# A WKV recurrence's state kept plain, with its two heads' products as two 64-row tiles

## The chip, the cores and the metric

The kernel runs on one core of a Trainium2 chip. The metric is the device time of one execution in microseconds, the median of several runs. The engines are TensorE (PE in the profile, its weight loads PEld), VectorE (DVE), ScalarE (ACT), GpSimd (POOL) and SyncE (SP, whose queue issues the DMAs). TensorE multiplies a stationary operand, loaded beforehand, with a moving one, into PSUM, which has eight banks. Its array of 128 rows by 128 columns can be divided into tiles of fewer rows (the contracted dimension, on the partitions) or columns; the profile writes the division as rows*columns.

## What is computed

A trunk of two layers on two sequences of 512 tokens with 1024 channels, in float32. Layer 0 is RWKV-7 time mixing with 16 heads of 64 channels, run forward and backward; layer 1 is a neighbourhood attention. The change concerns layer 0:

```python
def step(s, inp):                 # S is (batch, head, value, key)
    r_t, w_t, k_t, v_t, a_t, b_t = inp
    sa = jnp.einsum('bhvk,bhk->bhv', s, a_t)
    s = s * w_t[:, :, None, :] + sa[..., None] * b_t[:, :, None, :] + v_t[..., None] * k_t[:, :, None, :]
    return s, jnp.einsum('bhvk,bhk->bhv', s, r_t)
...
for d in range(2):
    xw = lerp(3 + d)
    xa = lerp(5 + d)
    w_log = -jax.nn.softplus(-(w0[d] + jnp.tanh(xw @ w1[d]) @ w2[d]).astype(f32)) - 0.5
    decay = heads(jnp.exp(-jnp.exp(w_log)))
    a = heads(jax.nn.sigmoid((a0[d] + (xa @ a1[d]) @ a2[d]).astype(f32)))
    k_d = k * (1.0 + (a - 1.0) * k_a_h)
    ys.append(_wkv7_scan(r, decay, k_d, v, -kk, kk * a, reverse=(d == 1)))
```

## The kernel before

The large products (`gemm`, L208 to L210) split each float32 operand into a high and a low part and add three products of 128x128 by 512 columns each. ACT and DVE or POOL make the parts (`halves`, L163 and L164).

The scan runs over eight blocks of four heads (two sequences, four blocks each), one after the other. A block is a chain of eight steps; a step is a chunk of 64 tokens of the forward direction and one of the backward direction (index `d`), for two pairs of heads (`g`) of two heads each (`h`). The two heads of a pair lie on partitions 0 to 63 and 64 to 127. In `scan_phase` the chain of one block runs beside the inverse of the next (`inverse`), the factors of the one after (`prep`), the end of the one before (`finish`) and the stream of large products (`stream`), in fixed shares of units. The order on each engine is then set by the framework's scheduler, and each engine works in that order.

What the change touches:

- `prep`, L475 and L476: the second, low-rank factor of decay and learning rate. `h` has the high parts of the hidden values on partitions 0 to 63 and the low parts on 64 to 127, `w2h` and `w2l` have the weights' high and low parts twice, one copy above the other. L475 multiplies 128 rows, L476 the upper 64 alone.
- `intra`, L619 to L671: what a step needs beside the state. It loads `ab` (tile `cab`: the factors a, b, k, r of four heads and both directions) and the values into `X`. ACT copies r into `Rb`, a tile of block-diagonal squares with zeros elsewhere (L637). POOL forms `bk` (L639). Then, for each direction and pair, TensorE multiplies in the whole array by `Rb` (L651), transposes `bk` (L654), and multiplies in quarters of the array for `AK` (L660, `TILES` gives the order of the quarters). DVE masks the results (L662, L665), ACT evacuates the transposes as `Tm` (L669). The PSUM tile `pf` is two banks; products with `Rb` lie in the first, transposes in the second, `AK`'s two heads in one each.
- `chain`, L673 to L756: the chain itself. The state of a pair is a block-diagonal square of 128 x 128 (`Sb`, two buffers, whose zeros are set once in `scan_phase`). A step multiplies it in the whole array (L697), adds the product of `AK` and the values (L702, half columns and half rows), copies the sums `Z` out of PSUM on ACT for direction 0 (L707) and on DVE for direction 1 (L708), multiplies by the inverse (L714), copies `X` (L716 on ACT, L717 on DVE), forms the state's increment (L722), adds it to the decayed state `WS` (DVE, L727, once for each head, and copies at L729 and L731 in the first step), forms the next `WS` (POOL, L736, once for each head), and adds the product of `R` and `X` to the outputs (L743), which ACT or DVE takes into `y` (L751, L753). The PSUM pool `zy` has two tiles of one bank, one for each direction; before the scan the large products use these banks.

Of the kernel before, what the change touches and what calls it, by code (L numbers as in the profile page):

```python
# [23 lines left out]
L = 64  # L24
# [24 lines left out]
class Trunk:  # L49
# [13 lines left out]
    NBK, NRB, NRR, NTM = 1, 2, 4, 4  # L63
# [103 lines left out]
    def sums(self, out, sel, x):  # L167
        """out = sel^T x, with sel of numbers that f32r has."""
# [12 lines left out]
    def operands(self, source):  # L181
        """The parts of KT tiles."""
# [7 lines left out]
    def weight(self, src):  # L190
        """The parts of KT blocks of P columns."""
# [10 lines left out]
    def gemm(self, w, x, tag):  # L202
        """Yields after every KT-th part; the value is the PSUM tile."""
# [11 lines left out]
    def sumsq(self, acc, x, k, eng=None):  # L215
        """Adds the squares of tile k."""
# [8 lines left out]
    def rstd(self, acc):  # L225
        """1 / sqrt(mean over the channels + eps) from the sums acc, on every partition; a PSUM tile."""
# [40 lines left out]
    def prelude(self, s):  # L267
# [5 lines left out]
        for k in range(KT):  # L273
# [5 lines left out]
            if s == 0:  # L279
                # without 1 / rms, which the products get  # L280
# [32 lines left out]
        # x w and x (mu w)  # L313
# [50 lines left out]
    def hidden(self, q, u):  # L364
        """High parts on partitions ..63, low parts on the others."""
# [17 lines left out]
    # ---------------------------------------------------------------- layer 0: r, k, v, z  # L383
    def columns(self, s, kind, x, ps=range(NP)):
        nc, sp = self.nc, self.sp
        vt, act = nc.vector, nc.scalar
        for p in ps:
# [3 lines left out]
            if kind == "z":  # L391
                # 2 silu(z)
# [21 lines left out]
            if kind == "v":  # L414
                # by token, forward and with the time reversed
# [24 lines left out]
    # ---------------------------------------------------------------- layer 0: factors of the chunks  # L440
    def prep(self, s, p):
        """Of two heads: k, a, b, r with the decays; A B^T of every chunk."""
# [26 lines left out]
        for d in range(2):  # L469
            ths = []  # L470
            for q, bias in ((d, 8 * d + p), (2 + d, 16 + 8 * d + p)):
# [4 lines left out]
                nc.tensor.matmul(ps, w2l[0:64, ws], h[0:64], start=False, stop=True)  # L476
# [20 lines left out]
            # by step of the chain, with the time reversed in the backward direction (r by token all the same);  # L497
            # of a step with e = 0: b, k, a, r, with e = 1: r, a, k, b
# [22 lines left out]
            # rows: e, half of the chunk, token; columns: the tokens of that half, then those of the other  # L521
# [68 lines left out]
        # on the first half of the tokens the inverse itself, on the second the product  # L590
# [28 lines left out]
    def intra(self, s, pb, i, wc):  # L619
        """Loads of a step, and what it needs of one chunk alone."""  # L620
# [9 lines left out]
        rb = self.Rb[self.nR % len(self.Rb)]  # L630
        self.nR += 1
        bk = None if last else t("bk", (P, 2, 2, 2, L), self.NBK)
        for d in range(2):
            self.load(ab[:, d].rearrange("p g a t -> p g (a t)"), sp["ab", s, pb][i][:, d])
            self.load(X[half(1 - e[d]), d].rearrange("p g h v -> p (g h v)"), sp["vt", s][i, pb, d].rearrange("t g c -> t (g c)"))
            for h in range(2):
                act.copy(rb[half(h), d, :, h], ab[half(h), d, :, 3 - 3 * e[d]])  # L637
# [5 lines left out]
        # R B^T and R K^T (R), B and K by token with the decay of the chunk (Tm), A K^T (AK)  # L643
        R, Tm = [], []
        AK = t("AK", (P, 2, 2, L), self.NAK)
        for d in range(2):
            fm = self.p("pf", (P, 2, T))
            f = fm[:, :, 0:256].rearrange("p x (g c) -> p x g c", g=2)
            for g in range(2):
                lhs = ab[:, d, g, 2 * e[d]:2 * e[d] + 2].rearrange("p a t -> p (a t)")  # L650
                nc.tensor.matmul(f[:, 0, g], lhs, rb[:, d, g].rearrange("p h t -> p (h t)"), start=True, stop=True)  # L651
            if not last:
                for g in range(2):
                    nc.tensor.transpose(f[:, 1, g], bk[:, d, g].rearrange("p a t -> p (a t)"), self.ident)  # L654
# [8 lines left out]
            h4 = lambda x: f[:, x].rearrange("p g (h t) -> p (g h) t", h=2)  # L663
            Rd = t("R", (P, 4, L), self.NRR)
            vt.tensor_tensor(Rd, h4(0), self.mr[d].unsqueeze(1).broadcast_to([P, 4, L]), op=ALU.mult)  # L665
            R.append(Rd.rearrange("p (g h) t -> p h g t", h=2))
            if not last:
                Td = t("Tm", (P, 4, L), self.NTM)
                act.copy(Td, h4(1))  # L669
                Tm.append(Td.rearrange("p (g h) t -> p h g t", h=2))  # L670
        return ab, X, R, Tm, AK  # L671

    def chain(self, s, pb, y):  # L673
        """The chain over the chunks, both directions at once.

        e = (step + direction) % 2 is the half of the partitions that has A S, Z and U of a direction; the other half has
        its V and outputs."""
# [9 lines left out]
        for i in range(NCH):  # L687
# [622 lines left out]
```

## Time and profile before

| | |
|---|---|
| median of 3 runs | 1995.89 us (1985.74 to 1996.47) |
| span of the profiled execution | 1996.9 us |
| mean granted clock of TensorE | 0.940 |
| packets of DMA, bytes | 219240, 333.88 MB |
| HBM read and written | 166 GB/s over the span |

The profile is of one execution. A row of a group gives the line in the kernel, the engine, the operation, the tiles (out<-in), the shapes, the number of instructions, busy time and mean duration of one, and the idle time of the engine just before them with what ended most of it. A float32 product with float32 operands stands as two instructions, a float32r product and a transpose as one. The end of a matmul is modelled and matmuls overlap, so the distance of starts tells more than a duration. A line of waits names the engine that waited and, behind the arrow, the instruction that ended the wait.

### The profile page before, as it was taken

The numbers are of one execution on the slowest core, as the hardware profiler recorded it, in microseconds if no ns is written. First come the engines' busy times: TensorE is split into PE (matmuls) and PEld (weight loads), VectorE is DVE, ScalarE is ACT, GpSimd is POOL, SyncE is SP. The second block draws the span as 40 slices with busy tenths as digits, with TensorE's granted clock in tenths as the row PEclk, the third lists the DMA queues.
The fourth block names the chain that finished last, engine by engine and source line by source line (L and its number), as shares of the span: only waits on it lengthen the run. The fifth ranks groups of instructions, "written<-read, shape, count | busy, mean of one in ns | idle before, by whom it ended". The sixth has DMA issues, their size and how long they took to land.

```text
span 1996.9 us, 41739 instructions
## 1 busy us (share of the span) xinstructions
PE 1834.5 (92%) x15968; PEld 1390.7 (70%) x15968; DVE 1330.7 (67%) x2513; ACT 1012.7 (51%) x2198; POOL 874.4 (44%) x996
## 2 busy tenths in 40 slices
PE   7899977899889899987998799999999999999998
PEld 5666655567667677765677677778777767777776
DVE  8977777765866867867668867343456666654563
ACT  4434555544544555553555444344357756555562
POOL 5544464643545634636347746223233316323232
PEclk9989987999888999997999889999999989999999
DMA  5426776644634756654456544344376424854562
GB/s 176 142 101 220 225 245 195 185 144 136 205 115 141 248 152 181 210 177 153 134 173 203 183 126 158 110 151 151 96 238 205 132 75 140 271 167 159 169 208 90
DMA packets 219240, 333.88 MB, mean 167 GB/s; under 512 B 20800, under 2 KB 86464, under 8 KB 219040
## 3 DMA queue, kind: packets, MB, share of 16 engines
q1 hardware_dynamic: 219040, 331.21, 52.5%
q8 instruction: 126, 2.06, 0.4%
q14 instruction: 74, 0.61, 0.1%
HBM read 225.61 MB, written 105.51 MB: 166 GB/s over the span
## 4 chain that ended last, share of the span: by engine, by line
PE 36%; DVE 6%; DMA 3%; ACT 2%; issue 2%; POOL 1%; SPq 0%; DVEq 0%; POOLq 0%; ACTq 0%
PE pg L208 5%; PE pg L210 4%; PE pg L209 4%; PE pm L208 2%; PE pm L209 2%; PE pm L210 2%; PE pm L940 2%; PE po L959 2%; PE pt L949 2%; PE pm L939 1%; PE zy L743 1%; PE pf L651 1%; PE zy L697 1%; PE zy L702 1%; DMA cab<-dab 1%
## 5 line engine op out<-in xcount | busy, mean ns | idle before, releaser
L164 POOL TENSOR_TENSOR wlo<-raw,whi 128x512 fp32r<-128x512 f32 x153 | 220.2, 1439 | 495.4 <-ACT whi L163 440.4
L163 ACT CAST whi<-raw 128x512 fp32r<-128x512 f32 x308 | 189.8, 618 | 197.5 <-PE pm L209 57.1
L208 PE MATMUL pm<-act,whi 128*128 128x512 f32 x520 | 225.7, 437 | 6.4 <-ACT tmp L897 1.8
L209 PE MATMUL pm<-act,whi 128*128 128x512 f32 x520 | 217.0, 417 | 2.4 <-DVE act L164 2.4
L210 PE MATMUL pm<-act,wlo 128*128 128x512 f32 x520 | 215.3, 414 | 3.6 <-POOL wlo L164 3.4
L164 DVE TENSOR_TENSOR wlo<-raw,whi 128x512 fp32r<-128x512 f32 x155 | 123.7, 798 | 126.7 <-ACT whi L163 124.1
L208 PE MATMUL pg<-act,whi 128*128 128x512 f32 x448 | 183.4, 411 | 0.0
L209 PE MATMUL pg<-act,whi 128*128 128x512 f32 x448 | 178.6, 399 | 1.3 <-DVE act L872 1.3
L210 PE MATMUL pg<-act,wlo 128*128 128x512 f32 x448 | 178.7, 400 | 0.1
L578 POOL TENSOR_TENSOR etmp<-N 128x30 f32<-128x30 f32 (+10 forms) x176 | 106.9, 607 | 63.6 <-DVE N L579 26.4
L208 PEld LDWEIGHTS pm<-act,whi 128*128 128x128 f32 x520 | 101.5, 196 | 41.5 <-issue 10.6
L210 PEld LDWEIGHTS pm<-act,wlo 128*128 128x128 f32 x520 | 102.4, 197 | 27.2 <-POOL wlo L164 3.9
L637 ACT COPY Rb<-cab 64x128 f32<-64x128 f32 x256 | 75.8, 296 | 88.7 <-DMA cab<-dab 85.5
L209 PEld LDWEIGHTS pm<-act,whi 128*128 128x128 f32 x520 | 102.8, 198 | 24.1 <-DVE act L164 4.1
L208 PE MATMUL zy<-act,whi 128*128 128x512 f32 x248 | 103.8, 424 | 16.4 <-ACT whi L163 9.0
L736 POOL TENSOR_TENSOR WS<-Sb,wc 64x256 f32<-64x256 f32 x96 | 71.5, 745 | 102.9 <-DVE Sb L727 86.7
L209 PE MATMUL zy<-act,whi 128*128 128x512 f32 x248 | 103.7, 418 | 13.8 <-DVE act L164 6.8
L639 POOL TENSOR_TENSOR bk<-cab,wc 128x256 f32<-128x256 f32 x112 | 78.8, 722 | 71.1 <-PE pf L654 46.4
L651 PE MATMUL pf<-Rb,cab 128*128 128x128 f32 x512 | 97.5, 313 | 12.9 <-ACT Tm L669 10.2
L579 POOL TENSOR_TENSOR N<-etmp,N 128x30 f32<-128x30 f32 (+10 forms) x176 | 104.1, 592 | 11.0
L210 PE MATMUL zy<-act,wlo 128*128 128x512 f32 x248 | 102.1, 412 | 1.0 <-DVE wlo L164 1.0
L208 PEld LDWEIGHTS pg<-act,whi 128*128 128x128 f32 x448 | 84.2, 189 | 20.8 <-issue 0.7
(380 smaller groups left out, 4551.3 us busy)
## 6 DMA issues: line engine op xcount, KB each, us to landing
dab<-ab SPq DMA_DIRECT2D x32, 1024.0 KB, 5.4
cab<-dab SPq DMA_DIRECT2D x128, 256.0 KB, 3.7
raw<-in_w_in_dram SPq DMA_DIRECT2D x128, 256.0 KB, 3.2
k<-dk SPq DMA_DIRECT2D x48, 256.0 KB, 4.1
bias<-in_rpb_dram SPq DMA_DIRECT2D x32, 384.0 KB, 3.9
raw<-in_w_z_dram SPq DMA_DIRECT2D x32, 256.0 KB, 3.7
dz<-tmp SPq DMA_DIRECT2D x32, 256.0 KB, 2.4
raw<-in_w_k_dram SPq DMA_DIRECT2D x32, 256.0 KB, 2.9
```

Source lines behind the costliest of these rows:

```text
L163: self.nc.scalar.copy(hi, src)
L164: (eng or self.nc.gpsimd).tensor_tensor(lo, src, hi.bitcast(F32), op=ALU.subtract)
L208: nc.tensor.matmul(ps, hi, x[k][0], start=(k == 0), stop=False)
L209: nc.tensor.matmul(ps, hi, x[k][1], start=False, stop=False)
L210: nc.tensor.matmul(ps, lo, x[k][0], start=False, stop=(k == KT - 1))
L578: eng.tensor_tensor(tv, N[:, q + 1:, q:q + 1].broadcast_to([P, n, q]), N[:, q:q + 1, :q].broadcast_to([P, n, q]), op=ALU.mult)
L579: eng.tensor_tensor(N[:, q + 1:, :q], tv, N[:, q + 1:, :q], op=ALU.add)
L637: act.copy(rb[half(h), d, :, h], ab[half(h), d, :, 3 - 3 * e[d]])
L639: gps.tensor_tensor(bk[:, d], ab[:, d, :, 2 * e[d]:2 * e[d] + 2], wc[:, d, :, i:i + 1].unsqueeze(3).broadcast_to([P, 2, 2, L]), op=ALU.mult)
L651: nc.tensor.matmul(f[:, 0, g], lhs, rb[:, d, g].rearrange("p h t -> p (h t)"), start=True, stop=True)
L736: gps.tensor_tensor(WS[half(h)].rearrange("p d g v -> p (d g) v"), Sn[half(h), :, :, h].rearrange("p d g v -> p (d g) v"), wcn, op=ALU.mult)
L940: nc.tensor.matmul(sc, Q[hs, h, qs], Kl[hs, ks], start=False, stop=True)
```

## The change

The state is a plain tile `S` with the keys of head 0 on partitions 0 to 63 and those of head 1 on 64 to 127. Every product of a whole pair becomes two, one for each head, which use 64 rows of the array and all its columns. The two heads write to different PSUM banks. `Rb` and `Sb`, with ACT's copies and the zeroing, go away. The addition to the state and the decayed state are each one instruction over both heads. `zy` becomes one tile of two banks for both directions, with a bank for each head; the two banks are given back when the scan begins and taken anew. `L476` multiplies 128 rows, so that the low part of the weights meets the low part of the hidden values as well. Comments are gone, and lines behind L637 move up by 3 to 8.

```diff
@@ prep
-                nc.tensor.matmul(ps, w2l[0:64, ws], h[0:64], start=False, stop=True)
+                nc.tensor.matmul(ps, w2l[:, ws], h, start=False, stop=True)
@@ intra
-        rb = self.Rb[self.nR % len(self.Rb)]
-        self.nR += 1
-            for h in range(2):
-                act.copy(rb[half(h), d, :, h], ab[half(h), d, :, 3 - 3 * e[d]])
...
-            f = fm[:, :, 0:256].rearrange("p x (g c) -> p x g c", g=2)
+            f = fm[:, :, 0:256].rearrange("p h (x g t) -> p h x g t", x=2, g=2)
             for g in range(2):
-                lhs = ab[:, d, g, 2 * e[d]:2 * e[d] + 2].rearrange("p a t -> p (a t)")
-                nc.tensor.matmul(f[:, 0, g], lhs, rb[:, d, g].rearrange("p h t -> p (h t)"), start=True, stop=True)
+                for h in range(2):
+                    nc.tensor.matmul(
+                        f[:, h, 0, g], ab[half(h), d, g, 2 * e[d]:2 * e[d] + 2].rearrange("p a t -> p (a t)"),
+                        ab[half(h), d, g, 3 - 3 * e[d]], start=True, stop=True)
             if not last:
                 for g in range(2):
-                    nc.tensor.transpose(f[:, 1, g], bk[:, d, g].rearrange("p a t -> p (a t)"), self.ident)
+                    for h in range(2):
+                        nc.tensor.transpose(
+                            f[:, h, 1, g], bk[half(h), d, g].rearrange("p a t -> p (a t)"), self.ident[half(h), 64 * h:64 * h + 64])
...
-            vt.tensor_tensor(Rd, h4(0), self.mr[d].unsqueeze(1).broadcast_to([P, 4, L]), op=ALU.mult)
+            vt.tensor_tensor(Rd, f[:, :, 0], self.mr[d].unsqueeze(1).unsqueeze(1).broadcast_to([P, 2, 2, L]), op=ALU.mult)
...
-                act.copy(Td, h4(1))
+                act.copy(Td, f[:, :, 1])
@@ chain
-            zy = [self.p("zy", (P, 2, 2, HD)) for d in range(2)]
+            zy = self.p("zy", (P, 2, T))[:, :, 0:256].rearrange("p h (d g v) -> p h d g v", d=2, g=2)
             if not first:
                 for d in range(2):
                     for g in range(2):
-                        lhs = ab[:, d, g, 2 - 2 * e[d]:4 - 2 * e[d]]
-                        nc.tensor.matmul(
-                            zy[d][:, g].rearrange("p h v -> p (h v)"), lhs.rearrange("p a t -> p (a t)"),
-                            S[:, d, g].rearrange("p h v -> p (h v)"), start=(g == 0), stop=False)
+                        for h in range(2):
+                            nc.tensor.matmul(
+                                zy[:, h, d, g], ab[half(h), d, g, 2 - 2 * e[d]:4 - 2 * e[d]].rearrange("p a t -> p (a t)"),
+                                S[half(h), d, g], start=(d == g == 0), stop=False)
...
-            act.copy(Z[half(e[0])], zy[0][half(e[0])])
-            vt.tensor_copy(Z[half(e[1])], zy[1][half(e[1])])
+            act.copy(Z[half(e[0])], zy[half(e[0]), :, 0])
+            vt.tensor_copy(Z[half(e[1])], zy[half(e[1]), :, 1])
...
-                for h in range(2):
-                    if not first:
-                        vt.tensor_tensor(Sn[half(h), :, :, h], so[half(h)], WS[half(h)], op=ALU.add)
-                    elif h:
-                        vt.tensor_copy(Sn[half(h), :, :, h], so[half(h)])
-                    else:
-                        act.copy(Sn[half(h), :, :, h], so[half(h)])
+                Sn = t("S", (P, 2, 2, HD), 2)
+                if first:
+                    vt.tensor_copy(Sn, so)
+                else:
+                    vt.tensor_tensor(Sn, so, WS, op=ALU.add)
...
-                    for h in range(2):
-                        wcn = wc.rearrange("p d g i -> p (d g) i")[half(h), :, i + 1:i + 2].broadcast_to([HD, 4, HD])
-                        gps.tensor_tensor(
-                            WS[half(h)].rearrange("p d g v -> p (d g) v"), Sn[half(h), :, :, h].rearrange("p d g v -> p (d g) v"),
-                            wcn, op=ALU.mult)
+                    gps.tensor_tensor(WS, Sn, wc[:, :, :, i + 1:i + 2].broadcast_to([P, 2, 2, HD]), op=ALU.mult)
...
-                        zy[d][half(1 - e[d]), g, h], R[d][:, h, g], X[:, d, g, h],
-                        start=(first and g == h == 0), stop=(g == h == 1))
+                        zy[half(1 - e[d]), h, d, g], R[d][:, h, g], X[:, d, g, h], start=False, stop=(g == 1),
+                        skip_group_check=True)
@@ scan_phase
-        self.Sb = [t(f"Sb{j}", (P, 2, 2, 2, HD)) for j in range(2)]
         self.MTb = [t(f"MT{j}", (P, 32, 2, 32)) for j in range(2)]
-        self.Rb = [t(f"Rb{j}", (P, 2, 2, 2, L)) for j in range(self.NRB)]
...
+        self.zs.close()
+        self.banks(mid, zy=1)
```

More of the change, by code (lines that the diff above doesn't have):

```diff
@@ L62 @@
     NAK, NZ = 1, 1
-    NBK, NRB, NRR, NTM = 1, 2, 4, 4
+    NBK, NRR, NTM = 1, 4, 4
     ELIM = (12, 20)
@@ L702, in chain @@
                     nc.tensor.matmul(
-                        zy[d][half(e[d]), g, h], AK[half(1 - e[d]), h, g], X[half(1 - e[d]), d, g, h],
-                        start=(first and g == h == 0), stop=(g == h == 1))
+                        zy[half(e[d]), h, d, g], AK[half(1 - e[d]), h, g], X[half(1 - e[d]), d, g, h],
+                        start=(first and g == 0), stop=(g == 1))
             yield
             Z = t("Z", (P, 2, 2, HD), self.NZ)
-            act.copy(Z[half(e[0])], zy[0][half(e[0])])
-            vt.tensor_copy(Z[half(e[1])], zy[1][half(e[1])])
+            act.copy(Z[half(e[0])], zy[half(e[0]), :, 0])
+            vt.tensor_copy(Z[half(e[1])], zy[half(e[1]), :, 1])
             us = self.p("us", (P, 2, 4, HD))
@@ L713, in chain @@
                     r = half(e[d])
-                    nc.tensor.matmul(u[r, g, h], mt[r, h, i, g], Z[r, g, h], start=True, stop=True)
+                    nc.tensor.matmul(u[r, g, h], mt[r, h, i, g], Z[r, h, g], start=True, stop=True)
             yield
@@ L743, in chain @@
                     nc.tensor.matmul(
-                        zy[d][half(1 - e[d]), g, h], R[d][:, h, g], X[:, d, g, h],
-                        start=(first and g == h == 0), stop=(g == h == 1))
+                        zy[half(1 - e[d]), h, d, g], R[d][:, h, g], X[:, d, g, h], start=False, stop=(g == 1),
+                        skip_group_check=True)
             for d in range(2):
@@ L750, in chain @@
                 if i < 4:
-                    act.copy(yi, zy[d][r])
+                    act.copy(yi, zy[r, :, d].rearrange("p h g v -> p g h v"))
                 else:
-                    vt.tensor_tensor(yi, zy[d][r], yi, op=ALU.add)
+                    vt.tensor_tensor(yi, zy[r, :, d].rearrange("p h g v -> p g h v"), yi, op=ALU.add)
             yield
@@ L1073, in stream, with scan_phase @@
             yield from self.inproj(0, self.xa, p)
-    def scan_phase(self, stream):
+    def scan_phase(self, stream, mid):
         todo, nul = self.todo, iter(())
         t = lambda tag, shape: self.t(tag, shape, 1, F32, self.front)
-        self.Sb = [t(f"Sb{j}", (P, 2, 2, 2, HD)) for j in range(2)]
         self.MTb = [t(f"MT{j}", (P, 32, 2, 32)) for j in range(2)]
-        self.Rb = [t(f"Rb{j}", (P, 2, 2, 2, L)) for j in range(self.NRB)]
-        self.nS = self.nM = self.nR = 0
-        for j in self.Sb + self.MTb + self.Rb:
+        self.nM = 0
+        for j in self.MTb:
             self.nc.gpsimd.memset(j, 0.0)
@@ L1145, in run @@
         stream = self.stream()
-        self.scan_phase(stream)
+        self.scan_phase(stream, mid)
         self.rest(stream, prep, mid)
```

15 lines of the change are left out of this document (7 added, 8 removed).

## The prediction

> **What bounds the kernel now.** I read the page first: busy shares and the forty slices of TensorE (PE) and of its granted clock.
>
> ```profile
> PE 1834.5 (92%) x15968; PEld 1390.7 (70%) x15968; DVE 1330.7 (67%) x2513; ACT 1012.7 (51%) x2198; POOL 874.4 (44%) x996
> ...
> PE   7899977899889899987998799999999999999998
> ...
> PEclk9989987999888999997999889999999989999999
> ```
>
> TensorE is busy nearly everywhere; no other engine is close. The recurrence, which the change rewrites, lies between about 350 and 1440 us (the rows of L697 and L714 below give first and last starts). The view by stages has the columns PE, PEld, DVE, ACT, POOL (each with its count), clock, DMA share, GB/s:
>
> ```profile
> 0.00:350.00 350.00, 298.04 (x1855) 218.29 (x1856) 271.84 (x387) 166.07 (x311) 170.60 (x189) 0.90 0.58 187
> 350.00:1440.00 1090.00, 995.56 (x11341) 763.19 (x11341) 730.86 (x1233) 522.03 (x1195) 519.36 (x673) 0.93 0.51 161
> 1440.00:1996.90 556.90, 540.85 (x2775) 409.17 (x2773) 327.98 (x894) 324.59 (x693) 184.46 (x134) 0.98 0.54 168
> ```
>
> In this stage TensorE is busy 995.6 of 1090 us, so 94.4 us are idle, at a clock of 0.93. Beside the chain, large products fill whatever TensorE has free, and their number is the same after the change. So the stage is as long as TensorE's work plus its waits, and the question is what the change does to each. ACT is busy 522 us there: an instruction saved on ACT counts only where TensorE waited for ACT.
>
> Then the waits of TensorE in that stage, longest first in total (total, times, longest):
>
> ```profile
> PE us L714 <- DVE Z L708: 18.5, 10, 4.1
> PE zy L697 <- DVE Sb L729: 10.5, 5, 4.3
> PE pf L651 <- ACT Tm L669: 10.2, 10, 2.1
> PE zy L697 <- DVE Sb L727: 8.0, 5, 2.5
> PE pm L802 <- DVE y L786: 4.9, 3, 2.4
> PE us L714 <- ACT Z L707: 4.6, 6, 1.9
> PE us L722 <- DVE X L717: 3.7, 4, 2.4
> PE zy L743 <- ACT X L716: 3.6, 9, 0.9
> ```
>
> No wait recurs at each of the 64 chain steps: the chain's latency is mostly covered by filler. That leaves TensorE's own work, so I read its instructions in order of time. A float32 product is two passes.
>
> ```profile
> 703.88 0.50 PE L475 MATMUL pm<-h,w2h 128*128 128x512 f32 x1
> 704.32 0.50 PE L476 MATMUL pm<-h,w2l 64*128 64x512 f32 x1
> 704.75 0.50 PE L208 MATMUL pm<-act,whi 128*128 128x512 f32 x1
> 705.09 0.39 PE L209 MATMUL pm<-act,whi 128*128 128x512 f32 x1
> 705.32 0.40 PE L210 MATMUL pm<-act,wlo 128*128 128x512 f32 x1
> 705.55 0.39 PE L208 MATMUL pm<-act,whi 128*128 128x512 f32 x1
> ```
>
> Products of 128x128 start 0.23 us apart (705.09, 705.32, 705.55). Into the 64x128 product of L476 it takes 0.44, out of it 0.43 (703.88, 704.32, 704.75). So a change of the array's division costs 0.20 us when the new tile has 128 columns. For 64 columns:
>
> ```profile
> 701.46 0.33 PE L743 MATMUL zy<-X,R 128*64 128x64 f32 x2
> 701.72 0.33 PE L660 MATMUL pf<-cab 64*64 64x64 f32 x2
> 701.97 0.33 PE L743 MATMUL zy<-X,R 128*64 128x64 f32 x2
> 702.23 0.32 PE L660 MATMUL pf<-cab 64*64 64x64 f32 x2
> ```
>
> Each two-pass product starts 0.255 us after the one before. Without a change two such passes take 0.124 (next fence), so this change costs 0.13.
>
> ```profile
> 685.98 0.68 PE L714 MATMUL us<-Z,MT 64*64 64x64 f32 x16
> ...
> 781.00 0.46 PE L660 MATMUL pf<-cab 64*64 64x64 f32 x16
> ...
> 706.25 1.05 PE L697 MATMUL zy<-Sb,cab 128*128 128x128 f32 x8
> ...
> L714 PE MATMUL us<-Z,MT x1024: 218/218/366, 364.0 to 1428.9; 64*64 64x64 f32 x171
> ...
> L697 PEld LDWEIGHTS zy<-Sb,cab x448: 186/192/338, 377.4 to 1422.7; 128*128 128x128 f32 x150
> L697 PE MATMUL zy<-Sb,cab x448: 270/275/582, 377.4 to 1422.8; 128*128 128x128 f32 x150
> ```
>
> The last three rows give min/median/max ns of one load or pass. L714 uses two tiles in turn: (0.68-0.218)/15 = 0.031 us a pass, 0.062 in one tile. L660 uses four: (0.46-0.218)/15 = 0.016. So tiles run side by side, row tiles with a PSUM bank each among them (L660 writes head h to bank h). L697 in the whole array: (1.05-0.275)/7 = 0.111.
>
> **The change part by part.**
>
> *Products by 64 rows (L651, L697).*
>
> ```profile
> L651 PE MATMUL pf<-Rb,cab 128*128 128x128 f32 x512 | 97.5, 313 | 12.9 <-ACT Tm L669 10.2
> ```
>
> Each step has four products of 8 passes in all at L651 and, but for the first step, at L697: 512/8 + 448/8 = 64 + 56 = 120 groups of 8 x 0.111 = 0.89 us. After it a group has 16 passes of half as many columns, on two row tiles. The stationary operand keeps its 128 columns. The first load after a change of division is exposed, and 0.20 against 0.13 above says that 128 columns load about 0.07 longer than 64; the whole-array pass of 0.111 streams as many columns as it loads. If the load sets the pace, a tile takes 0.111 a pass and the pair 16 x 0.111 / 2 = 0.89: nothing gained. Bounds: the pair at L714's rate, 16 x 0.031 = 0.50, is 120 x 0.39 = 47 us less; no overlap, 16 x 0.111 = 1.78, is 107 us more. I take 0, because a 128-column load is in every pass of L697 too, and L660 shows overlap.
>
> [...]
>
> *Transposes (L654).*
>
> ```profile
> 780.68 0.38 PE L654 MATMUL pf<-cc,bk 128*128 128x128 f32 x2
> ...
> L654 PEld LDWEIGHTS pf<-cc,bk x224: 137/142/230, 351.9 to 1408.2; 128*128 128x128 f32 x112
> L654 PE MATMUL pf<-cc,bk x224: 270/273/421, 352.0 to 1408.3; 128*128 128x128 f32 x112
> ```
>
> One pass each, 0.38-0.273 = 0.11 apart: 224 x 0.11 = 25 us. After: 448 in pairs at L714's 0.031 = 14; unpaired at 0.062 = 28. Their loads are short (142 ns against the 192 of L697 in the fence before), so here the load need not set the pace: I take -10 (bounds -11 and +3).
>
> *Changes of division.* This is the largest term. L651, L654 and L697 stood in the same division as the large products around them and could join them without a change; as 64x128 products they cannot. I counted, in the built order of TensorE's instructions (it holds no times), how often neighbours differ in division:
>
> ```
> into a tile of            before   low-rank part alone   after
> 128 columns                  764                   669     828
> 64 columns                   474                   474     632
> 32 columns or the row sums   228                   228     320
> all                         1466                  1371    1780
> ```
>
> The low-rank part (L476 on 128 rows) saves 95 x 0.20 = 19 us. The rest adds 159 x 0.20 + (158 + 92) x 0.13 = 64 us, the 32-column ones at the price of 64. Together +45. Part of it is that the new order cuts the small products up more: the runs of L743, L660, L702, L714, L722 go from 540 to 709. A run can end on a product without its pair, 169 x 0.062 = 10 at most; I take +5.
>
> TensorE's work: 0 - 10 + 45 + 5 = +40 us at full clock, 40/0.93 = +43 at the granted one.
>
> *What leaves the other engines.*
>
> ```profile
> L637 ACT COPY Rb<-cab 64x128 f32<-64x128 f32 x256 | 75.8, 296 | 88.7 <-DMA cab<-dab 85.5
> ...
> L736 POOL TENSOR_TENSOR WS<-Sb,wc 64x256 f32<-64x256 f32 x96 | 71.5, 745 | 102.9 <-DVE Sb L727 86.7
> ...
> L727 DVE TENSOR_TENSOR Sb<-us,WS x96: 377/422/430, 393.2 to 1417.9; 64x256 f32<-64x256 f32 x96
> ...
> L708 DVE COPY Z<-zy x64: 404/422/429, 364.3 to 1423.8; 64x256 f32<-64x256 f32 x64
> ```
>
> ACT loses 75.8 us of copies into Rb and the 85.5 us in which its queue stood at such a copy until the DMA of cab had landed, with casts and evacuations behind it. POOL loses 48 of 96 products (36 us), DVE half of its additions (48 x 0.42 = 20 us). All that is covered by TensorE's work, except where TensorE waited. The new S is whole after one DVE instruction, not two: 0.42 earlier in the ten waits for Sb, -4. ACT ended 18.4 us of the quoted waits (10.2 + 4.6 + 3.6); I take half, -9, for its freed queue; bounds 0 and about -30, all of ACT's and the ten for Sb.
>
> *What is added.* The zy tile is one for both directions. In the built order DVE's copy of Z (L708), which waited for TensorE alone, now waits for ACT's copy (L707), as X's (L717) did already. It starts up to one copy later, and DVE's queue stands behind it. TensorE's 16 waits for Z get 0.42 longer: +7; bound 64 x 0.42 = +27. A step's products with S wait for both outputs' evacuation; such waits are not among the longest, so nothing. Opening zy anew after the first stage happens once: nothing.
>
> Sum against the profiled execution, whose span of 1996.9 us is 1 us above the runs' median: 1996.9 + 43 - 4 - 9 + 7 = 2034 us, 1.9% slower. Its own range: 2034 - 30 (relief at its bound, fewer changes felt) to 2034 + 46 (Z at its bound with the DVE queue behind it, a quarter of the overlap lost): 2004 to 2080.
>
> **The rivals.**
>
> *The freed queues win (faster).* The place is the stage's 94.4 idle us and its clock of 0.93. If ACT's queue, no longer stopped by DMA, and the shorter way to S took half of the idle time (47) and with it half of the clock's loss (0.07 x 1090 / 2 = 38), the time would be 1996.9 + 43 - 85 = 1955. It decides from the point where the relief passes 43 us. For it: 85.5 us of ACT standing. Against it: the quoted waits that ACT or Sb ended are 37 us, and Z's wait gets longer.
>
> *The pairs run at 64-column pace.* 47/0.93 = 51 less: 2034 - 51 = 1983. For it: L714's 0.031; against it: the load. [...]
>
> *The row tiles do not overlap.* 107/0.93 = 115 more: 2149. Against it: L660's 0.016 on four tiles.
>
> *The changes of division fall into waits.* TensorE drains where it would have waited for S or Z anyway; the 94 idle us could hold the 43. Then nothing is seen: about 1997. Against it: the waits are few and long, the changes many and everywhere.
>
> **How the numbers follow.** Forecast 0.56; freed queues 0.18; 64-column pace 0.09; no overlap 0.07; hidden changes 0.10. Half a per cent, 10 us, is what a measurement tells from no change. Faster: 0.18 and most of 0.09, 0.25; same: 0.10 and the edges of the neighbours, 0.12; slower 0.63. The range goes from 1968, into the freed queues' case, to 2085, leaving out the missing overlap and the deep end of the relief.
>
> **What would show it.** TensorE's busy time in the stage up by about 40 us with L648 (the former L651) and L697 at about the former busy time or a little above; pairs of starts in L697 0.11 us apart (0.06 would be the 64-column pace, single starts 0.11 apart no overlap); products next to a change 0.13 to 0.20 late; L475 and L476 0.23 apart; ACT's wait for cab gone; DVE's copy of Z behind ACT's. The prediction is wrong if TensorE's idle time in the stage falls by more than 40 us, or if its busy time does not rise.

## The result and the profile after

The changed kernel takes 2146.36 us (median of 4 runs, 2142.92 to 2149.43) against 1994.58: a ratio of 1.0788, 95% interval 1.0752 to 1.0825. That is 152 us slower; the prediction was 2034 us, at most 2085. Each later run was measured beside the kernel before, whose median then lay between 1990.94 and 1995.53 us. The profiled execution has a span of 2147.6 us, 151 above that of before. From the page, the busy shares of TensorE and the granted clock:

```profile
PE 1972.6 (92%) x17152; PEld 1495.4 (70%) x17152; DVE 1312.4 (61%) x2465; ACT 942.5 (44%) x1938; POOL 833.2 (39%) x944
...
PE   7899887899898898898899879999999999999998
...
PEclk9899986878778678796678877999999989999999
```

TensorE is as busy as before, 92%. The row of the clock is what differs: mostly 6, 7 and 8 tenths through the recurrence where there was mostly 8 and 9. The view by stages of the changed kernel, cut where its recurrence ends (columns as in the prediction's):

```profile
0.00:350.00 350.00, 292.04 (x1855) 219.09 (x1856) 271.16 (x387) 163.80 (x304) 169.54 (x185) 0.90 0.57 186
350.00:1595.00 1245.00, 1143.71 (x12535) 868.28 (x12534) 709.97 (x1183) 455.55 (x942) 476.69 (x625) 0.81 0.44 141
1595.00:2147.60 552.60, 536.85 (x2765) 408.07 (x2763) 331.22 (x897) 323.10 (x693) 187.00 (x134) 0.98 0.53 168
```

The whole loss is in the recurrence, 1245 us against 1090. A stage can be split into three: TensorE's idle time, its busy time times the granted clock (an estimate of the work at full clock; in the pairs alone, below, a pass took 0.214 us at 0.50 and 0.111 at 1.00), and the rest of its busy time, which the clock costs. Before: idle 94.4, work 995.6 x 0.93 = 926, clock 70. After: idle 101.3, work 1143.7 x 0.81 = 926, clock 217. The clock's two decimals make these uncertain by some 6 us. So in these two executions work and idle time are nearly what they were, and about 147 of 155 us are the clock. (What "work" can tell between kernels is less than that; the last experiment comes back to it.)

The clock's own records in the two traces hold only two values, 0.50 and 1.00. In the recurrence before there are 26 stretches at 0.50, 147 us in all; after the change there are 35, 464 us in all. So the clock fell somewhat more often, and it stayed down for 13 us on average in place of 6.

The products themselves, in order of time, at a place of full clock (L648 is the former L651, L735 the former L743; L697 to L727 keep their numbers):

```profile
1351.51 0.39 PE L208 MATMUL pm<-act,whi 128*128 128x512 f32 x1
1351.74 0.39 PE L209 MATMUL pm<-act,whi 128*128 128x512 f32 x1
1351.97 0.39 PE L210 MATMUL pm<-act,wlo 128*128 128x512 f32 x1
1352.29 1.11 PE L697 MATMUL zy<-S,cab 64*128 64x64 f32 x16
1353.32 0.45 PE L702 MATMUL zy<-X,AK 64*64 64x64 f32 x8
...
L697 PE MATMUL zy<-S,cab x896: 272/272/473, 382.8 to 1580.5; 64*128 64x64 f32 x180
```

Sixteen passes of L697 in 1.11 - 0.272 = 0.84 us of starts: 0.056 a pass, 0.112 a pair. The two row tiles do run side by side, at the pace of a tile that loads 128 columns and not at the 0.062 us of L714, which loads 64. A group takes what the whole-array group took.

TensorE's waits in the stage, longest first:

```profile
PE us L714 <- ACT Z L707: 16.8, 9, 4.9
PE us L722 <- DVE X L717: 14.8, 8, 3.9
PE us L714 <- DVE Z L708: 14.1, 5, 6.3
PE pf L648 <- ACT Tm L669: 9.5, 5, 3.3
PE zy L735 <- ACT X L716: 8.6, 6, 2.5
PE zy L697 <- DVE S L727: 4.8, 2, 3.5
```

The waits for the state fell (18.5 to 4.8 us in the lines shown), those for Z and X rose (Z from 23.1 to 30.9, X from 7.3 to 23.4). ACT's wait for the DMA of cab, 85.5 us, is gone from its list, but ACT stands as long elsewhere. The first line is of the kernel before, the others of the changed one:

```profile
ACT Tm L669 <- DVE R L665: 91.4, 59, 8.4
...
ACT Tm L669 <- DVE R L665: 187.9, 76, 8.2
ACT Z L707 <- PE zy L702: 90.2, 41, 14.7
```

### The profile page after: what moved, and what is told of

The parts are those of the page before. It is cut to its first block, busy times and chain, and to the rows that moved or that the text cites. A ratio compares the mean times of both kernels' runs of the same rounds, so it can differ in the third digit from the quotient of the medians.

```text
span 2147.6 us, 43756 instructions
## 1 busy us (share of the span) xinstructions
PE 1972.6 (92%) x17152; PEld 1495.4 (70%) x17152; DVE 1312.4 (61%) x2465; ACT 942.5 (44%) x1938; POOL 833.2 (39%) x944
## 4 chain that ended last, share of the span: by engine, by line
PE 61%; DVE 18%; DMA 6%; POOL 6%; ACT 4%; issue 4%; SPq 1%; DVEq 0%; ACTq 0%; POOLq 0%
PE pm L208 5%; PE pg L208 5%; PE pg L210 4%; PE pg L209 4%; PE pm L209 4%; PE pm L210 4%; PE pf L648 3%; PE zy L697 3%; PE zy L735 2%; DVE MT L588 2%; PE zy L702 2%; PE pf L661 2%; PE us L714 2%; PE pm L606 2%; PE pm L932 2%
## 5 line engine op out<-in xcount | busy, mean ns | idle before, releaser
L208 PE MATMUL pm<-act,whi 128*128 128x512 f32 x520 | 242.2, 467 | 4.7 <-ACT th L478 2.8
L209 PE MATMUL pm<-act,whi 128*128 128x512 f32 x520 | 234.6, 451 | 4.3 <-POOL act L164 2.2
L210 PE MATMUL pm<-act,wlo 128*128 128x512 f32 x520 | 231.1, 444 | 2.7 <-POOL wlo L164 2.7
L208 PEld LDWEIGHTS pm<-act,whi 128*128 128x128 f32 x520 | 110.8, 213 | 36.5 <-issue 5.1
L210 PEld LDWEIGHTS pm<-act,wlo 128*128 128x128 f32 x520 | 111.7, 215 | 30.1 <-POOL wlo L164 3.2
L209 PEld LDWEIGHTS pm<-act,whi 128*128 128x128 f32 x520 | 111.6, 215 | 28.6 <-DVE act L164 2.6
L578 POOL TENSOR_TENSOR etmp<-N 128x30 f32<-128x30 f32 (+10 forms) x176 | 98.5, 560 | 76.4 <-DVE N L572 38.4
L669 ACT COPY Tm<-pf 128x256 f32<-128x256 f32 x112 | 41.6, 371 | 195.9 <-DVE R L665 187.9
L648 PE MATMUL pf<-cab 64*128 64x64 f32 x1024 | 112.1, 323 | 10.2 <-ACT Tm L669 9.5
L730 POOL TENSOR_TENSOR WS<-S,wc 128x256 f32<-128x256 f32 x48 | 32.6, 678 | 212.8 <-DVE S L727 173.7
L648 PEld LDWEIGHTS pf<-cab 64*128 64x128 f32 x1024 | 88.8, 220 | 30.5 <-ACT Tm L669 11.9
```

The costliest lines, as they stand in the source:

```text
L208: nc.tensor.matmul(ps, hi, x[k][0], start=(k == 0), stop=False)
L209: nc.tensor.matmul(ps, hi, x[k][1], start=False, stop=False)
L210: nc.tensor.matmul(ps, lo, x[k][0], start=False, stop=(k == KT - 1))
L578: eng.tensor_tensor(tv, N[:, q + 1:, q:q + 1].broadcast_to([P, n, q]), N[:, q:q + 1, :q].broadcast_to([P, n, q]), op=ALU.mult)
L648: nc.tensor.matmul(f[:, h, 0, g], ab[half(h), d, g, 2 * e[d]:2 * e[d] + 2].rearrange("p a t -> p (a t)"), ab[half(h), d, g, 3 - 3 * e[d]], ...
```

## The experiments

The question was why the clock fell. Three theories stood:

- **Clock theory.** It supposes that the granted clock follows how much of the array streams. A whole-array pass on a block-diagonal square streams 128 columns through all 128 rows, zeros included, and the next one starts 0.111 us later. A pair of 64-row passes streams 64 columns on each tile in 0.112 us: by the estimate below, the array stands half empty. 120 groups of 0.89 us, 107 of 926 us of work, go from full to half.
- **Division theory.** It supposes that the 1780 changes of division instead of 1466, each 0.13 to 0.20 us by the prediction's rows, cost time and clock.
- **Wait theory.** It supposes that DVE's copy of Z behind ACT's stops TensorE, and that the clock falls with the idle time.

How full a pass is can be estimated from a product of the kernel before that has only 2 columns to load (82 ns a load):

```profile
381.48 1.02 PE L408 MATMUL pm<-tmp,cc 128*2 128x512 f32 x2
```

One of the two passes lasts 0.59 us, so they start 1.02 - 0.59 = 0.43 us apart. If that is the streaming of the 512 columns, 128 take 0.107. By this estimate a pass of 128 columns every 0.111 us streams 0.96 of the time, one of 64 columns 0.48.

**One part alone: the low-rank product.**

```diff
 # the kernel before
-                nc.tensor.matmul(ps, w2l[0:64, ws], h[0:64], start=False, stop=True)
+                nc.tensor.matmul(ps, w2l[:, ws], h, start=False, stop=True)
```

> The kernel before with the low-rank product on 128 rows and nothing else. The built order has 1371 changes of division, 95 fewer than before. Priced at 0.20 us each: 19 us less, 1970 to 1985 us against 1995. Clock theory (TensorE's clock falls where the array is half empty): the product fills the array now, so the clock rises a little above 0.94 as well. If low-rank were part of the 151 us, this would be slower than before.

Measured: 1990.42 us against 1993.96, ratio 0.9995 (0.9966 to 1.0024). It is no part of the loss, and no gain that the measurement tells apart. Its stage:

```profile
350.00:1430.00 1080.00, 983.41 (x11327) 764.42 (x11325) 732.06 (x1230) 522.50 (x1194) 518.25 (x672) 0.93 0.51 161
```

Work 983.4 x 0.93 = 915: in this execution the work is 11 us less, where 95 changes fewer were priced at 19, and no such gain can be told in the median.

**The half-empty tiles filled.** In the changed kernel each product with r and with the state streams both pairs' columns; the second 64 go to unused columns of the PSUM bank.

```diff
 # the changed kernel; the same at L648 with ab and fm
+            zyf = self.p("zy", (P, 2, T))
-                                zy[:, h, d, g], ab[...]
-                                S[half(h), d, g], start=(d == g == 0), stop=False)
+                                zyf[:, h].rearrange("p (b t) -> p b t", t=HD)[:, 2 * d + g::4][:, 0:2], ab[...]
+                                S[half(h), d, ::-1] if g else S[half(h), d], start=(d == g == 0), stop=False)
```

> The changed kernel, but each 64-row product with r and with the state streams 128 columns in place of 64, the second 64 into unused columns of its PSUM bank that nobody reads. A load of 128 columns takes as long as the longer stream, so the products' pace stays. Clock theory: the two tiles are full again, the clock in the recurrence's stage goes from 0.79 to 0.88 or more, and the time to 2010 to 2060 us. Division theory (the drains of 1780 changes of division against 1466 cost time and clock): this order has 1607 changes, so at most half of the loss comes back, about 2070; by the price of a change alone, 2120. Wait theory (DVE's copy of Z behind ACT's): 2146 as in the changed kernel.

Measured: 2059.75 us, ratio 1.033 (1.0296 to 1.0365). By the median, 87 of 152 us come back by streaming twice the columns. The row of the clock in its page, and its stage:

```profile
PEclk9899986899898899896798799999999999999999
```

```profile
350.00:1510.00 1160.00, 1026.71 (x12528) 779.36 (x12525) 708.54 (x1180) 454.70 (x940) 477.90 (x623) 0.89 0.48 151
```

Idle 133.3, work 914, clock 113. The clock's cost fell from 217 to 113, though this kernel waits more than the changed one. 173 changes of division fewer are 22 to 35 us at the 0.13 to 0.20 us a change of the prediction's rows, and the division theory expected about 2070 at the least. The time is still 66 us above the kernel before. The transposes, 448 passes, still stream 64 columns on 64 rows here.

**Another order.** The output products are issued ahead of the next step's loads.

```diff
 # the changed kernel: L733 to L745 moved in front of L731
+            (products of R and X, evacuation into y)
             if not last:
                 nxt = self.intra(s, pb, i + 1, wc)
                 yield
```

> The changed kernel, but a step's output products are issued ahead of the next step's loads and products; the built order has 1660 changes of division against 1780. Division theory: the 314 extra changes cost 151 us, 120 of them go, so about 2090 us. Clock theory: the half-empty products stay, clock about 0.87 over the span, 2110 to 2150 us.

Measured: 2155.32 us, ratio 1.0816 (1.0758 to 1.0874). 120 changes of division less gave no shorter time, where the division theory expected about 2090. The stage shows why this is weaker than it looks:

```profile
350.00:1595.00 1245.00, 1100.60 (x12523) 838.88 (x12522) 712.52 (x1181) 451.54 (x939) 483.11 (x624) 0.82 0.44 141
```

Idle 144.4, work 902, clock 198. The work is 24 us less than in the changed kernel, as much as 120 changes at 0.20 us, and the idle time is 43 us more. So a gain of that size may lie under new waits. The clock's loss stays within 19 us of the changed kernel's, as the clock theory expected.

**The plain state alone.** `intra`, `Rb` and the low-rank product are those of before; `chain` is the changed one.

```diff
 # the changed kernel with intra (L619 to L671) and L476 of before, and
+        self.Rb = [t(f"Rb{j}", (P, 2, 2, 2, L)) for j in range(2)]
```

> The kernel before with the plain state alone (products with the state by 64 rows, one zy tile, one addition); the products with r, the transposes and the low-rank product as before. The built order has 1435 changes of division, fewer than the 1466 of before. Division theory: not slower than before, 1985 to 1997 us. Clock theory: 56 of the 120 groups are half empty, so about half of the loss: clock about 0.90 to 0.91, 2050 to 2080 us. Wait theory (Z's copies in sequence): the whole loss, about 2140.

Measured: 2067.43 us, ratio 1.0369 (1.0321 to 1.0417), with 1435 changes of division, fewer than before. The stage:

```profile
350.00:1520.00 1170.00, 1021.83 (x11798) 773.15 (x11797) 698.66 (x1183) 522.92 (x1186) 472.87 (x625) 0.87 0.48 150
```

Clock 133, work 889, idle 148. The clock's cost rises by 63 us with 56 of 120 groups half empty. But the idle time rises too, by 54, so here it isn't the half-empty groups alone that can have lowered the clock.

**One zy tile alone.** To see the wait by itself, the kernel before gets one zy tile for both directions.

```diff
 # the kernel before
-            zy = [self.p("zy", (P, 2, 2, HD)) for d in range(2)]
+            zyf = self.p("zy", (P, 2, T))
+            zy = [zyf[:, d, 0:256].rearrange("p (g h v) -> p g h v", g=2, h=2) for d in range(2)]
 # and the two banks are given back and taken anew before the scan, as in the changed kernel
```

> The kernel before with one zy tile of two banks for both directions (a bank each), and nothing else: DVE's copy of Z now waits for ACT's, and the next step's products for both outputs. Full-array products stay. Wait theory: this is what remained of the loss in the run with doubled columns (2060 us), so 2040 to 2060 us, idle TensorE time in the stage 30 to 50 us above the 94 of before. Clock theory alone: no half-empty products, 1990 to 2005 us.

Measured: 2006.99 us against 1991.19, ratio 1.0083 (1.0054 to 1.0113).

```profile
350.00:1460.00 1110.00, 987.09 (x11353) 754.95 (x11353) 719.36 (x1231) 523.67 (x1197) 512.97 (x673) 0.90 0.49 158
```

```profile
PE us L715 <- DVE Z L709: 22.6, 13, 5.9
PE pf L651 <- ACT Tm L669: 19.8, 17, 2.6
PE us L715 <- ACT Z L708: 13.2, 12, 2.7
```

Idle 122.9 (28 more) and clock 99, work 888. The wait for Z is 35.8 us against 23.1. So the joined tile, together with the new order it brings (1362 changes of division in its trace, 104 fewer), costs 16 us by the median, about a tenth of the loss. The idle time rose nearly as the wait theory expected (30 to 50), the time did not (2040 to 2060).

**Half the columns in the kernel before.** The reverse of the second experiment, with the whole-array product and its load left as they are:

```diff
 # the kernel before
-                            zy[d][:, g].rearrange("p h v -> p (h v)"), lhs.rearrange("p a t -> p (a t)"),
-                            S[:, d, g].rearrange("p h v -> p (h v)"), start=(g == 0), stop=False)
+                            zy[d][:, g, 0], lhs.rearrange("p a t -> p (a t)"),
+                            S[:, d, g, 0], start=(g == 0), stop=False)
```

> The kernel before, but the whole-array product with the block-diagonal state streams 64 columns in place of 128: the head 0 half. It leaves out the state's part of head 1 of each pair. The load of 128 columns still sets the pace, or the products get shorter. Clock theory: half of the array time of 56 of 120 groups is gone, and the clock falls as with the plain state alone: 0.90 to 0.92 over the span, 2020 to 2060 us, although work is left out. Division theory (1553 changes against 1466): 87 x 0.15 = 13 us more, 2007. If neither holds, 1995 or less, since 25 us of streaming are left out.

Measured: 2032.16 us, ratio 1.0201 (1.0146 to 1.0255).

```profile
350.00:1460.00 1110.00, 1017.15 (x11326) 780.73 (x11326) 739.65 (x1230) 524.55 (x1193) 516.27 (x672) 0.91 0.49 158
```

Idle 92.9 and work 926 are those of before, clock 92 against 70. A kernel that leaves work out is 41 us slower by the median. Its profiled execution, 2018.8 us long, is faster than its median, and the clock there (0.929 over the span) is a little above the 0.90 to 0.92 expected. Its clock cost is no more than that of the mere reorder below (91), so of this run only the median, 41 us against the reorder's 19, speaks for the clock theory.

**The products with r alone, half empty and full.** `intra` of the changed kernel in the kernel before, without `Rb`; then the same with 128 streamed columns and the low-rank product on 128 rows.

```diff
 # the kernel before with intra of the changed one; then, in addition:
+                    rr = ab[half(h), d, :, 3 - 3 * e[d]]
-                        f[:, h, 0, g], ab[...], ab[half(h), d, g, 3 - 3 * e[d]], start=True, stop=True)
+                        fm[:, h].rearrange("p (b t) -> p b t", t=L)[:, g::6][:, 0:2], ab[...],
+                        rr[:, ::-1] if g else rr, start=True, stop=True)
```

> The kernel before with the products with r and the transposes as 64-row pairs, the copies into Rb gone, and state, zy and low-rank product as before. Clock theory: 64 of 120 groups half empty and no new wait: clock 0.90 to 0.92, 2040 to 2070 us. Wait theory: no wait is added and ACT is freed, so 1985 to 1997 us. Division theory (1659 changes): 193 x 0.15 = 29 us more, 2025.

> The run before this one with 128 streamed columns in each product with r, so that both tiles are full, and the low-rank product on 128 rows. Clock theory: the clock is back at 0.93 to 0.94, 1980 to 2010 us. Division theory (1602 changes): 2015.

Measured: 2040.44 us, ratio 1.0247 (1.0201 to 1.0293), and 2027.3 us, ratio 1.0175 (1.0146 to 1.0204). The stages of the first and the second:

```profile
350.00:1487.00 1137.00, 1051.63 (x12027) 802.02 (x12028) 717.40 (x1228) 453.58 (x944) 511.44 (x671) 0.88 0.48 153
```

```profile
350.00:1468.00 1118.00, 1022.19 (x12005) 788.62 (x12006) 735.85 (x1226) 451.71 (x941) 512.86 (x670) 0.91 0.48 155
```

The first is the cleanest case: ACT is freed of 75 us of copies, TensorE's idle time is 85.4 (9 less than before), its work 925, as before, and still it loses 49 us at the median, with a clock cost of 126 against 70. Filling the tiles brings the clock's cost to 92 and the time 13 us down. In both traces the clock falls 29 times in the stage; it stays at 0.50 for 273 us in the first and for 201 us in the second. The gain is less than expected (1980 to 2010); 36 us above the kernel before stay unexplained by this pair.

**The clock by itself.** Behind the last output of the kernel before, TensorE stands idle for 17 us and then runs nothing but 64-row products:

```diff
 # the kernel before, behind last()
+        pairs(140, 64)            # 64 columns on both row tiles
+        pairs(134, 128)           # 128 columns on both
+        pairs(180, 64)
+        pairs(200, 128, (0,))     # one row tile
+        pairs(200, 64, (0,))
```

> The kernel before with a tail behind its last output that nobody reads: TensorE idle for about 20 us, then 140 pairs of 64-row products of 64 columns on two row tiles, 134 pairs of 128 columns, 180 pairs of 64 again, 200 products of 128 columns on one row tile, 200 of 64 columns on one row tile. Clock theory, with the share of the array's cells times time as what counts: the first pairs (0.48 of it, the load being twice the stream) start at half clock after the idle time and stay there, a pair of two passes each about 0.22 us apart; the full ones (0.96) bring the clock to 1.0 within about 10 us; the second 64-column pairs keep it at 1.0 (0.48 doesn't let it fall); one tile of 128 columns (0.48) keeps it; one tile of 64 columns (0.24) lets it fall to 0.5. [...] Overlap: a pair takes 0.11 us a pass at full clock; without overlap 0.22.

The view by stages, one row for each part (length, TensorE busy, weight load busy, three engines, clock, DMA share, GB/s):

```profile
1995.00:2054.90 59.90, 59.81 (x562) 59.81 (x562) 0.04 (x1) 0.00 (x0) 0.00 (x0) 0.50 0.00 1
2054.90:2086.20 31.30, 31.30 (x540) 31.30 (x540) 0.00 (x0) 0.00 (x0) 0.00 (x0) 0.96 0.01 2
2086.20:2126.30 40.10, 40.10 (x724) 40.10 (x721) 0.00 (x0) 0.00 (x0) 0.00 (x0) 1.00 0.01 2
2126.30:2171.00 44.70, 44.70 (x404) 44.70 (x403) 0.00 (x0) 0.00 (x0) 0.00 (x0) 1.00 0.00 1
2171.00:2253.60 82.60, 82.60 (x401) 82.60 (x400) 0.00 (x0) 0.00 (x0) 0.00 (x0) 0.52 0.00 1
```

TensorE is busy in nearly every microsecond of it, 258.51 of 258.60. The first pairs, behind 17 us without work, stay at 0.50 for 60 us: 280 passes a tile in 59.9 us, 0.214 each. Over the full pairs the clock averages 0.96, in 31.3 us. The same 64-column pairs that had stayed at half clock now stay at 1.00, 360 passes in 40.1 us, 0.111 each. One tile of 128 columns, by the estimate half the array all the time, stays at 1.00 too (400 passes in 44.7 us, 0.112). One tile of 64 columns, by the estimate a quarter of the array's time, has 0.52 (400 passes in 82.6 us). So in this one execution busy time does not set the clock: TensorE is busy for 59.81 of 59.90 us at 0.50 and for 40.10 of 40.10 at 1.00. Nor does the count of instructions: 400 passes in one tile have 1.00 with 128 columns and 0.52 with 64. By the estimated fill, 0.48 of the array had 0.50 behind the idle time and 1.00 behind the full pairs, and 0.24 had 0.52. More than these five stretches the run does not show. The tail has no product of 128 rows, so that such a pass counts for two of 64 rows rests on the kernels and not on it.

**More of the array at another place.** On top of the low-rank product alone, each product of `AK` runs a second time on the idle quarters.

```diff
 # the kernel before with the low-rank product on 128 rows; zy tiles of 512 columns, zx their second half
+                for d in range(2):
+                    nc.tensor.matmul(
+                        zx[d][half(1 - e[d]), g, h], AK[half(1 - e[d]), h, g], X[half(1 - e[d]), d, g, h],
+                        start=(first and g == h == 0), stop=(g == h == 1), skip_group_check=True)
```

> The run with the low-rank product alone (1990 us against 1994), and each product of AK with the values a second time into unused columns of its PSUM bank, on the two quarters of the array that lay idle beside it. Clock theory: 512 products go from half to all of the array at the same pace, the clock rises from 0.936 by about 0.01 and the time falls by 5 to 15 us, to 1975 to 1990 us. Otherwise the 512 further products cost something: 1995 to 2020 us.

Measured: 2028.76 us against 1990.94, ratio 1.0187 (1.0138 to 1.0235). A miss: slower, not faster. Stage and first wait:

```profile
350.00:1466.00 1116.00, 1004.25 (x12344) 779.46 (x12344) 729.83 (x1228) 524.08 (x1193) 513.76 (x671) 0.91 0.49 156
```

```profile
PE zy L749 <- ACT X L722: 28.4, 17, 5.1
```

Work 914 and idle 111.8; TensorE's wait for ACT's X is 28.4 us where it was 3.6 before. The clock theory expected a higher clock than the 0.93 of the run with the low-rank product alone; it is 0.91. The further products also moved the order and added waits; whether the fuller quarters brought anything beneath that, this run does not show.

**What another order alone does.** One unit more of large products beside the first chain; and other shares with the low-rank product.

```diff
 # the kernel before; the second with the low-rank product on 128 rows
-    PACE = (57, 57, 57, 57, 55, 70, 75, 55)
+    PACE = (58, 57, 57, 57, 55, 70, 75, 55)
...
+    PACE = (55, 56, 57, 57, 56, 70, 75, 55)
```

> The kernel before with 58 instead of 57 units of large products beside the first block's chain: the same instructions in a slightly other order (1445 changes of division against 1466). This measures what another order alone does. If order alone moves the time by 20 us or more, the run with full quarters (2029 us) and the rest in the run with full r pairs (2027 us) can be that; if it stays within 10 us of 1991, those two need a cause of their own.

> The low-rank product on 128 rows with shares of 55, 56, 57, 57, 56, 70, 75, 55 units in place of 57, 57, 57, 57, 55, 70, 75, 55; 1355 changes of division. Division price of 0.20 us: 111 fewer changes than before, 1970 to 1980 us, faster than both kernels. Clock theory with the order's noise: 1980 to 2005 us, not told apart from the kernel before.

Measured: 2014.1 us against 1995.53, ratio 1.0075 (1.0047 to 1.0103); and 1991.69 us, ratio 0.9974 (0.9956 to 0.9992). The first does nothing but reorder, and is 19 us slower:

```profile
350.00:1465.00 1115.00, 1015.93 (x11384) 784.34 (x11383) 738.03 (x1240) 536.42 (x1209) 530.02 (x675) 0.91 0.50 158
```

Idle 99.1, work 924, clock 91 against 70. So a new order alone can cost 20 us, nearly all of it clock. Differences of that size, as with the joined zy tile, half of what the full r pairs left and much of the miss with full quarters, are not to be read as effects of the edit itself. The second has the lowest ratio of all runs here, a quarter of a per cent under the kernel before. Its stage:

```profile
350.00:1440.00 1090.00, 994.07 (x11341) 776.57 (x11340) 731.85 (x1234) 530.37 (x1202) 535.44 (x673) 0.91 0.51 161
```

Five kernels have as many matrix products as the kernel before, on other orders: itself (1466 changes of division), this reorder (1445), the low-rank product (1371), the joined tile (1362) and this last one (1355). Their work is 926, 924, 915, 888 and 905 us. So an order moves the work by up to 38 us, and the orders with some 100 changes fewer have 11 to 38 us less of it, which the prediction's price of 0.20 us a change would put at 20. Little of that came out in the medians; in the last, the clock costs 89 us against 70.

## Why the prediction was wrong

- *What bounds the kernel.* Right. TensorE's work, waits and clock make up the stage, and ACT's 75 us and the DMA waits of its queue brought nothing in the time (9 us less idle time where they alone were taken away).
- *Products by 64 rows: nothing gained.* Right for TensorE's pace: 0.112 a pair. It went with the load: in the pairs alone, at clock 1.00, a pass in one tile took 0.111 us with 64 columns streamed and 0.112 with 128, all with 128 columns loaded. The rival in which the tiles do not overlap gave 2149 us, almost the number measured, and is false by the 0.112. A number that fits does not show its cause.
- *The failed step* is "40/0.93 = +43 at the granted one". It took the clock of the recurrence as given and divided by it. The change moved the clock itself, from 0.93 to 0.81 in the stage, worth about 147 us. In the pairs alone an array half filled by the estimate, busy for 59.81 of 59.90 us, did not bring the clock back from 0.50. Doubled columns, at the same loads, brought back 104 of the 147 us of clock and 87 of the 152 us, and the products with r alone lost 49 us with less idle time than before. The prediction had counted equal time as equal work: 16 half-filled passes for 8 full ones, "nothing gained", while the time the array was filled was, by the estimate, halved (0.96 to 0.48).
- *Changes of division, +45.* Open. The changed kernel's work is that of before, 926 us, where the sum had 40 more. But work differs by up to 38 us between orders of the same products, and there fewer changes go with less work. So the price may be right and something else in the changed kernel may have saved as much, such as the transposes in pairs; no run here took that apart. In the time, 95, 111 and 120 changes fewer gave at most a quarter of a per cent.
- *Waits.* Right for Z, +8 us (predicted +7); the state's fell by 14 (predicted 4). X's rose by 16, where the sum had no rise. Idle time in all is 7 us more instead of 6 less, a small error beside the clock's.
- *Freed queues* did not win. The three waits that ACT ended, of which the sum took half away, grew from 18.4 to 34.9 us, while ACT stood 187.9 us for DVE's R at L669 instead of 91.4.
- *The signs of being wrong* that the prediction named did not show it: the idle time did not fall by 40 us, and the busy time rose, by 148 us, but through the clock.

What stays open: the changed kernel with doubled columns is still 66 us above the kernel before, of which the joined tile can be 16 and a new order about 20; full r pairs are 36 us above it, with the same 20; and by how much waits, as against half-filled passes, lowered the clock in the run with the plain state alone. So that half-filled passes cost clock in these kernels is shown (0.81 in the stage, 0.89 with the columns doubled; 0.88 with the products with r half empty, 0.91 with them full and the low-rank product on 128 rows), and the exact part of the 147 us that they cost is not.

## What to carry to other kernels

Count what part of the array streams, not only how long TensorE is busy: here a padded whole-array product took 0.111 us a pass where two half-filled tiles took 0.112, and the clock of the stage was 0.93 with the first and 0.81 with the second. The row tiles gained no time, with 128 columns loaded in each (0.112 us); a tile of L714, with 64 columns to load, took 0.062. In a kernel whose order a scheduler sets, measure what reordering alone does before a difference of one per cent is put down to an edit.

## What was not expected of the hardware

The same product had two clocks. In the pairs alone the same pairs of 64 columns ran for 60 us at 0.50 after an idle time and for 40 us at 1.00 after full pairs, so in that execution their clock went with what stood before them. If the half-filled products of the recurrence keep the clock they find, which is the author's supposition, a fall there would last until something filled the array, and 107 us of half-filled work may so have cost 147 us of clock. The clock records fit this: 26 falls became 35, but the time at 0.50 went from 147 to 464 us, so most of the loss is in how long the clock stayed down. Which products kept it down each time was not taken apart.
